# The seam into the last feed-forward stage: three engines' order written down, and some half weights in an idle staging tile

## The chip, the cores and the metric

The kernel runs on one core of a Trainium2 chip. The metric is the device time of one execution in microseconds. TensorE (PE) multiplies matrices, ScalarE (ACT), VectorE (DVE) and GpSimd (POOL) do the rest of the arithmetic, and SyncE (SP) issues most of the transfers; POOL issues the others.

## The reference

Two layers of a diffusion backbone over 1024 latent tokens of width 1024 and 256 context tokens, in float32. Layer 0 mixes with Fourier groups and long convolutions, layer 1 with neighbourhood attention; each ends with a gated feed-forward part. What matters here is the end of layer 1:

```python
def swiglu(u, w_gate, w_up, w_down):
    return (jax.nn.silu(u @ w_gate) * (u @ w_up)) @ w_down

y_lat, y_ctx = mixer_na(u_lat, u_ctx, na_w_qkv[j], na_w_out[j], na_rpb[j], not last)
h_lat = h_lat + g1 * y_lat
h_lat = h_lat + g2 * swiglu(modulate(rms_norm(h_lat, norm2_g[i]), sh2, sc2),
                            ffn_w_gate[i], ffn_w_up[i], ffn_w_down[i])
...
return rms_norm(h_lat, final_g)
```

`mixer_na` projects to queries, keys and values (the latent tokens and the keys and values of the context), attends, and multiplies by `na_w_out`. The feed-forward width is 2816, eleven pairs of 128-column blocks in each of gate and up.

## The kernel before

**Numbers.** An activation or a weight is split into two float16 tiles, a high and a low half, and a product takes three matmuls: high by high, high by low, low by high. TensorE does a 128x512 piece per matmul.

**The feed-forward products.** Gate and up products run by Strassen's scheme in Winograd's form: a 2x2 block product in seven products, A11·B11, A12·B21, S1·T1, S2·T2, S3·T3, A22·T4 and S4·B22. A and S come from the weights, B and T from the activations. Each product has four blocks of the inner dimension, so twelve matmuls. `wino_steps` is a generator that yields after each product; `Steps.to(n)` runs one to its n-th product. After products 1, 4 and 5 ScalarE copies a sum out of PSUM (`snap`); after 2, 5 and 7 VectorE adds to it. Pair i of the hidden blocks has a gate chain `g` and an up chain `up`.

**The activations' operands.** B11 and B21 come from the first half of the tokens and are there early (`wino_first`, in tiles `s4`). The others need the second half and its RMS factor: `wino_second` scales a block by that factor (`scaled`), subtracts (T1, T2, T3, T4), and makes the two halves: the high one by a cast on ScalarE, the low one by a subtraction on VectorE (`out`). It yields after each block, twenty in all, in the order T1, T2, T3, T4, B22. The high and low tiles are named `s4`, as the float32 blocks are named `s2`.

**The weights.** A pair's weights arrive in float32 in the staging tile `ws` (two buffers of 128x1024) and in others; `abs_sums` takes absolute sums on ScalarE, TensorE adds these over partitions (a 128x1 matmul), and from the scale `half_split` makes `wh` and `wl` (two buffers each). Of pairs 0 and 1 of layer 1 the halves are ready in DRAM (`d`) and are loaded to `wh` and `wl`, and S operands to `s2`. Pair 2, the third, is the first to be split there.

**The stages around the change.** After layer 0 comes the attention, whose first key weights are loaded as halves into `wh`/`wl` (`halves_of("wk", 0)`). The output projection with `na_w_out` (`w_out2`) runs as `first_part(pc)`, the first six inner blocks for token half pc, eight output blocks nb of eighteen matmuls, and `last_part(pc)`, the two remaining; `add_h` adds the residual, `square` squares and sums for the RMS norm. The seam is what follows `last_part(1)`: `rms_begin(1)` sums the squares over the partitions (small matmuls), `rms_end` makes the factor, spreads it with two matmuls and copies it to SBUF. Four chains are begun there (gate and up of pairs 0 and 1), and then `ffn` runs.

**What sets the order.** A scheduler orders the instructions of each engine from the program's text, its dependencies and its own estimate of times, and semaphores keep the data right; each engine runs its own order in sequence. Pools give buffers: a tile's load waits until the earlier tenant of its buffer has been read.

Of the kernel before, what the change touches and what calls it, by code (L numbers as in the profile page):

```python
# [12 lines left out]
F16 = mybir.dt.float16  # L13
BF16 = mybir.dt.bfloat16
AF = mybir.ActivationFunctionType
# [4 lines left out]
P = 128  # L20
# [181 lines left out]
class Builder:  # L202
    def __init__(self, ctx, tc, a, out, taps=None, stop=None):
        self.tc, self.nc, self.a, self.out = tc, tc.nc, a, out
        self.taps, self.stop = taps, stop
        ent = ctx.enter_context
        self.cp = ent(tc.tile_pool(name="cp", bufs=1))
        self.p4 = ent(tc.tile_pool(name="p4", bufs=20))
        self.p2 = ent(tc.tile_pool(name="p2", bufs=34))
        self.pg = ent(tc.tile_pool(name="pg", bufs=4))  # L210
        self.pt = ent(tc.tile_pool(name="pt", bufs=6))
        self.pko = ent(tc.tile_pool(name="pk", bufs=4))
        self.pw = ent(tc.tile_pool(name="pw", bufs=2))
        self.psum = ent(ExitStack())
        self.accumulators(pp=6, pq=2)
        self.dr = ent(tc.tile_pool(name="dr", bufs=1, space=bass.MemoryType.DRAM))
        self.pad(self.cp, PAD_C)
        self.k = self.mk = self.pk = 0
        self.banks = 8
        self.sq, self.wsc, self.uslot, self.ahead = {}, {}, {}, {}  # L220

    def pad(self, pool, w):
# [1037 lines left out]
    def abs_sums(self, tiles, st):  # L1260

        junk = self.T(BF16, 1024)
        for k, t in enumerate(tiles):
            self.nc.scalar.activation(junk[:, :t.shape[1]], t, AF.Abs, scale=2.0 ** -15, accum_out=st[:, k:k + 1])  # L1264

    def qkv_sums(self):

# [81 lines left out]
    def wino_second(self, h, l, m, r):  # L1349

        nc = self.nc
        dsh = self.C(4)
        ad = self.ucol[0]
        nc.vector.tensor_tensor(dsh, ad[:, 4:8], ad[:, 0:4], SUB)

        def out(key, j, src):
            hi, lo = self.pair((key, j))
            nc.scalar.copy(hi, src)
            nc.vector.tensor_tensor(lo, src, hi, SUB)

        ts = []

        def scaled(b):
            t = h.ap(0, b, 1)
            nc.vector.scalar_tensor_tensor(t, t, ad[:, 8 + b:9 + b], r, op0=MUL, op1=MUL)
            return t

        for j in range(4):
            t11, t21 = self.raw.pop(j), self.raw.pop(j + 4)
            t12 = scaled(j)  # L1370
            nc.vector.tensor_tensor(t11, t12, t11, SUB)
            out("T1", j, t11)
            ts.append([t11, t12, None, t21])
            yield
        for j in range(4):
            ts[j][2] = t22 = scaled(j + 4)
            t11 = ts[j][0]
            sh = ad[:, j + 4:j + 5]
            nc.vector.scalar_tensor_tensor(t11, t22, sh, t11, op0=ADD, op1=SUB)
            out("T2", j, t11)  # L1380
            yield
        for j in range(4):
            t11, t12, t22, t21 = ts[j]
            nc.vector.scalar_tensor_tensor(t12, t22, dsh[:, j:j + 1], t12, op0=ADD, op1=SUB)
            out("T3", j, t12)
            yield
        for j in range(4):
            t11, t12, t22, t21 = ts[j]
            sh = ad[:, j + 4:j + 5]
            nc.vector.scalar_tensor_tensor(t21, t21, sh, t11, op0=ADD, op1=SUB)  # L1390
            out("T4", j, t21)
            yield
        for j in range(4):
            t22 = ts[j][2]
            sh = ad[:, j + 4:j + 5]
            hi, lo = self.pair(("B22", j))
            nc.scalar.activation(hi, t22, AF.Identity, bias=sh)
            nc.vector.scalar_tensor_tensor(lo, t22, sh, hi, op0=ADD, op1=SUB)
            yield

# [91 lines left out]
        self.res = {(0, 0): c11, (0, 1): c12, (1, 1): c22, (1, 0): pa}  # L1492
        yield

    def wino_begin(self, l, i, m, tile, ctile=None):

        key = (l, i, m)
        w = self.first_ahead(key)
        s = Steps(self.wino_steps(w, tile, ctile))
        s.w, s.whole = w, False  # L1500
        s.to(2)
        return s

    def ffn(self, l, u, h, hs, second, after, keep=None, begun={}):
# [67 lines left out]
        def fetch(i, m):  # L1572
            b = begun.get((i, m))
            if i < n2 and (b is None or not b.whole):
                g = self.weights_ahead((l, i, m), b.w) if b else self.wino_weights((l, i, m))
                next(g)
                waiting[(i, m)] = g

        fetch(0, 0)
        for i in range(n2):  # L1580
            g, up = begun.get((i, 0)), begun.get((i, 1))
            if g is None or not g.whole:
                wg = waiting.pop((i, 0))
                w = next(wg)
                next(wg)
            fetch(i, 1)
            if g is None:
                g = Steps(self.wino_steps(w, self.G))
                g.to(1)
            if prev is not None:  # L1590
                prev[0].to(7)
                finish(i - 1, prev[1])
            wu = waiting.pop((i, 1))
            w = next(wu)
            if up is None:
                up = Steps(self.wino_steps(w, self.TK))
            if i == 0:
                for k, _ in enumerate(second):
                    if k == 11:
                        next(wu)  # L1600
            next(wu, None)
            fetch(i + 1, 0)
            for k in (3, 4, 5) if i == 0 and l == 1 else ():
                g.to(k)
                up.to(k)
            g.to(5)
            up.to(1)
            if i == n2 - 1:
                scales = self.down_scales(l, nh)
                if l == 0:  # L1610
                    self.qkv_scales()
            g.to(7)
            gate = dict(self.res)
            inv = self.wsc[(l, i, 0)][1]
            for k in ((0, 0), (1, 1), (0, 1)):
                nc.scalar.activation(gate[k], gate[k], AF.Silu, scale=inv)
            t = self.G()
            nc.scalar.activation(t, gate[(1, 0)], AF.Silu, scale=inv)
            gate[(1, 0)] = t
            up.to(5)  # L1620
            prev = (up, gate)
            for k in (2 * i - 2, 2 * i - 1) if l == 1 else (9, 10) if i == 9 else (i,) if i < 9 else ():
                if 0 <= k < n2:
                    sums(k)
            for _ in range(2):
                next(todo, None)
# [234 lines left out]
        for _ in range(3):  # L1861
            yield w

    def halves_of(self, n, b):

        t = [self.pw.tile([P, 1024], F16, tag=g, name=self.nm(g)) for g in ("wh", "wl")]
        for k, x in enumerate(t):
            self.ld(x, self.halves[(n, b)][:, k * 1024:(k + 1) * 1024])
        return t
# [38 lines left out]
    def attn_prep(self, pr, u):  # L1908
# [68 lines left out]
            vt.append((v, lo))  # L1977

        acc = None
        wk = self.halves_of("wk", 0) if pr == 0 else self.aw  # L1980
        for pc in (0, 1, 2):
            if pc == 1:
                wq = self.halves_of("wq", pr)
# [191 lines left out]
    def run(self):  # L2175
# [228 lines left out]

        def first_part(pc):
            for nb in range(KB):
                wh, wl = (self.pw.tile([P, 1024], F16, tag=g, name=self.nm(g)) for g in ("wh", "wl"))
                for k, x in enumerate((wh, wl)):
                    self.ld(x[:, :768], self.halves[("w_out2", nb)][:, k * 1024:k * 1024 + 768])
                if pc == 0:  # L2410
                    yield None
                acc = self.PQ() if pc == 0 else self.PS()
                for kb in range(6):
                    if pc == 0 and nb == 0:
                        load_o(kb, (0,), self.ld)
                        yield 1
                    if pc == 0 and nb == 2:
                        load_o(kb, (1,), self.ld)
                    if kb == 2:
                        load_h2(nb, pc)  # L2420
                    for w, part in ((wh, 0), (wh, 1), (wl, 0)):
                        self.mm(acc, w[:, kb * P:(kb + 1) * P], by_row(o.ap(part, kb, pc)),
                                kb == 0 and w is wh and part == 0, kb == 5 and w is wl)
                    yield 0.5
                add_h(nb, pc, acc)
# [53 lines left out]
            nc.scalar.activation(sq[:, c0:c0 + 256], h4.ap(0, KB - 1, pc), AF.Square)  # L2479
            yield from scale_out(pc, self.rms_end(pc, self.rms_begin(pc, [self.sq[1][0], sq], c0), False))  # L2480

        begun = {(0, 0): self.wino_begin(1, 0, 0, self.G)}
        c = self.rms_begin(1)
        begun[(0, 1)] = self.wino_begin(1, 0, 1, self.TK)
        r1 = self.rms_end(1, c)
        begun[(1, 0)] = self.wino_begin(1, 1, 0, self.G, self.TK)
        begun[(1, 1)] = self.wino_begin(1, 1, 1, self.TK, self.S2)
        self.ffn(1, None, h4, hs1, self.wino_second(h2, 1, 3, r1), after4, begun=begun)


def host_layout(i):
# [75 lines left out]
```

## Time and profile before

| | us |
|---|---|
| median of three runs | 2901.01 |
| lowest, highest | 2895.24, 2902.95 |
| profiled execution | 2897.71 |
| its span | 2895.6 |
| TensorE busy in it | 2758.4 (95%) |
| VectorE, ScalarE, GpSimd busy | 2081.9, 1620.2, 593.0 |

The mean granted clock of TensorE was 0.978 of full speed. A row of a timeline gives start, duration, engine, line, operation and tiles (out<-in), shape and count, and in brackets how long the engine stood before it and what released it. `SPq` is a transfer issued by SP. Lines are those of the kernel before; in the kernel after the same lines stand 1 to 26 further down.

### The profile page before, as it was taken

The page shows a single profiled execution, that of the slowest core. Times are in us where ns is not written, and L with a number is a line of the kernel's source. Part 1 is how long each engine was busy: PE and PEld are TensorE (multiplying, and loading weights), DVE is VectorE, ACT ScalarE, POOL GpSimd, SP SyncE. Part 2 cuts the span into 40 slices and gives each one's busy share as a digit, 9 for nine tenths or more (in the row PEclk, how much of TensorE's full clock was granted, in tenths as well). Part 3 has the DMA queues.
Part 4 walks back from the last instruction along what each step waited for, and adds up shares of the span by engine and source line. Part 5 has one row for each costly group of instructions (what it writes and reads, how often), then busy time and mean ns, then how long its engine had stood idle before and what let it go on. Part 6 is the DMA issues. An engine that isn't in the chain of part 4 may idle for free. (4 is left out here: it accounts for less than half of the span.)

```text
span 2895.6 us, 46377 instructions
## 1 busy us (share of the span) xinstructions
PE 2758.4 (95%) x16419; PEld 1688.7 (58%) x16419; DVE 2081.9 (72%) x3857; ACT 1620.2 (56%) x2857; POOL 593.0 (20%) x977
## 2 busy tenths in 40 slices
PE   6989999999989999999999999999999899999998
PEld 3766557878879644444555844666664444444554
DVE  4778867585467798877886777777775778775755
ACT  4664325453675666654555555666663567554543
POOL 1012013354220111123120012343321112112000
PEclk8989999999999999999999999999999999999999
DMA  7574435358785655566995698777864756425753
GB/s 257 191 275 161 159 124 159 109 165 293 279 342 177 211 209 196 201 221 219 315 336 193 238 330 333 167 170 167 177 186 166 248 199 246 151 95 184 237 190 117
DMA packets 323363, 607.60 MB, mean 210 GB/s; under 512 B 89910, under 2 KB 131576, under 8 KB 323130
## 3 DMA queue, kind: packets, MB, share of 16 engines
q1 hardware_dynamic: 254682, 387.53, 41.6%
q0 software_dynamic: 66144, 212.91, 20.8%
q10 hardware_dynamic: 2304, 4.20, 0.4%
q8 instruction: 129, 2.11, 0.3%
q14 instruction: 104, 0.85, 0.1%
HBM read 455.33 MB, written 135.53 MB: 204 GB/s over the span
## 5 line engine op out<-in xcount | busy, mean ns | idle before, releaser
L1462 PE MATMUL ps<-s,s 128*128 128x512 f16 x2244 | 507.3, 381 | 8.9 <-ACT g L1467 4.7
L1462 PEld LDWEIGHTS <-s 128*128 128x128 f16 x2640 | 258.7, 98 | 332.3 <-issue 26.8
L296 PE MATMUL ps<-s,wh 128*128 128x256 f32 (+3 forms) x1764 | 402.3, 331 | 12.1 <-ACT wh L300 5.7
L1231 ACT ACTIVATE s<-s,c 128x512 f16<-128x512 f32 (+1 forms) x324 | 233.2, 752 | 147.3 <-DMA s<-d 71.4
L1232 DVE SCALAR_TENSOR_TENSOR s<-s,c,s 128x512 f16<-128x512 f32 (+1 forms) x324 | 247.3, 792 | 87.0 <-ACT s L1231 85.9
L1679 PE MATMUL ps<-s 128*128 128x512 f16 (+2 forms) x1308 | 303.8, 378 | 2.3 <-DVE s L1232 2.0
L296 PE MATMUL pq<-s,wh 128*128 128x512 f16 (+1 forms) x988 | 271.4, 352 | 5.0 <-DMA wh<-d 3.0
L296 PE MATMUL ps<-s,wl 128*128 128x256 f32 (+3 forms) x882 | 264.4, 332 | 2.6 <-DMA wl<-d 1.6
L1679 PEld LDWEIGHTS <-s 128*128 128x128 f16 x1536 | 148.4, 98 | 179.5 <-issue 7.4
L296 PEld LDWEIGHTS <-wh 128*128 128x128 f16 x1664 | 159.1, 99 | 151.1 <-issue 12.2
L287 POOL DMA_DIRECT2D d<-s x201 | 108.6, 541 | 652.2 <-DVE s L1523 186.1
L348 ACT CAST mat<-cs 128x1024 fp32r<-128x1024 f16 (+2 forms) x120 | 111.5, 934 | 140.5 <-PE ps L296 53.5
L296 PEld LDWEIGHTS ps<-s,wh 128*128 128x128 f32 x1088 | 178.3, 193 | 18.4 <-ACT wh L300 5.9
L296 PE MATMUL ps<-s,mat 128*128 128x512 f32 x696 | 183.1, 410 | 3.1 <-DVE s L302 2.8
L1462 PE MATMUL ps<-s,wh 128*128 128x512 f16 x608 | 182.3, 379 | 1.6 <-DVE g L1476 1.2
L296 PE MATMUL pq<-s,wl 128*128 128x512 f16 (+1 forms) x494 | 171.2, 352 | 0.0
L296 PEld LDWEIGHTS <-s 128*128 128x128 f16 x2400 | 113.6, 98 | 80.7 <-issue 12.8
L296 PEld LDWEIGHTS ps<-s,mat 128*128 128x128 f32 x696 | 135.7, 197 | 37.1 <-DVE s L302 3.2
L1264 ACT ACTIVATE t<-s 128x1024 bf16<-128x1024 f32 (+1 forms) x164 | 141.5, 864 | 13.4 <-DVE c L483 8.6
L296 PE MATMUL sc<-s,s 128*128 128x65 f16 (+3 forms) x2688 | 142.6, 231 | 3.2 <-ACT t L2080 2.4
L296 PEld LDWEIGHTS <-wl 128*128 128x128 f16 x832 | 81.8, 99 | 81.2 <-DMA wl<-d 2.5
L1231 ACT ACTIVATE s<-t,c 128x512 f16<-128x512 f32 x172 | 115.2, 712 | 21.9 <-DVE c L1330 9.3
(435 smaller groups left out, 5505.9 us busy)
## 6 DMA issues: line engine op xcount, KB each, us to landing
s<-d SPq DMA_DIRECT2D x294, 256.0 KB, 4.2
d<-s POOLq DMA_DIRECT2D x157, 256.0 KB, 3.7
s<-in_down SPq DMA_DIRECT2D x154, 256.0 KB, 5.0
s<-in_ada_w POOLq DMA_DIRECT2D x48, 512.0 KB, 4.9
s<-in_gate SPq DMA_DIRECT2D x46, 512.0 KB, 4.0
s<-in_up SPq DMA_DIRECT2D x46, 512.0 KB, 3.8
d<-g POOLq DMA_DIRECT2D x87, 256.0 KB, 3.4
d<-tk POOLq DMA_DIRECT2D x82, 256.0 KB, 4.9
```

The source lines that it names most:

```text
L287: self.last_ldr = self.nc.gpsimd.dma_start(out, in_).ins
L296: return self.nc.tensor.matmul(o, l, r, start=st, stop=sp).ins
L348: self.nc.scalar.copy(m, st)
L1231: nc.scalar.activation(hi, src, AF.Copy, scale=scale)
L1232: nc.vector.scalar_tensor_tensor(lo, src, scale, hi, op0=MUL, op1=SUB)
L1264: self.nc.scalar.activation(junk[:, :t.shape[1]], t, AF.Abs, scale=2.0 ** -15, accum_out=st[:, k:k + 1])
L1462: nc.tensor.matmul(ps, x[:, sl], y, start=first and j == 0 and x is wh and y is xh, stop=j == 3 and x is wl, skip_group_check=True)
L1679: m = nc.tensor.matmul(acc[j][:, c0:c1], x[:, sl], y[:, xs], start=first and k == 0, stop=last and k == 2, skip_group_check=True)
```

## The change

**Staging tile.** The key weights of the attention's first head pair, and the halves of `w_out2` for even nb in `first_part(1)`, go to a buffer of the tag `ws`, high half in its first 1024 columns and low half in the others. The transfers of SP move with the buffers. SP ahead of the attention, before (`d_3522` holds the first key weights, `d_3526` the first query weights, `in_gate` and `in_up` the float32 weights of the third pair):

```order
L281 DMA ws_5399_25751<-in_gate 128x1024
L281 DMA s4_3749_17455<-in_up 128x1024
L281 DMA s4_3750_17456<-in_up 128x1024
L281 DMA ws_5433_25949<-in_up 128x1024
L281 DMA wl_3815_17559<-d_3522_16515 128x1024
L281 DMA wh_3814_17558<-d_3522_16515 128x1024
```

and after (`d_3644` holds `w_out2`'s block 0):

```order
L282 DMA ws_3814_17558<-d_3522_16515 128x1024 x2
L282 DMA s4_3749_17455<-in_up 128x1024
L282 DMA s4_3750_17456<-in_up 128x1024
L282 DMA ws_5024_24831<-d_3644_16969 128x768 x2
L282 DMA wl_3819_17599<-d_3526_16522 128x1024
L282 DMA wh_3818_17598<-d_3526_16522 128x1024
```

The key weights stand where the first staging load stood, and the two staging loads `ws<-in_gate` and `ws<-in_up` have moved behind `first_part(1)`'s last load and into `last_part(1)`'s. At the start of the attention the scheduler also puts ScalarE's first value cast behind the context keys' scores; the steady part of the attention reads as before.

**Seam.** From the first of the four chains to the end of pair 0's gate activation the order on PE, ACT and DVE is that of the program's text, not the scheduler's. The text runs the RMS chain between product 1 and product 2 of the first gate chain, gives one block of `wino_second` at a time between the products, and then S1·T1 of gate and up, S2·T2 of both, S3·T3 of both with further blocks between. The low half of a block is subtracted one block later than its cast. `abs_sums` keeps behind the last cast of B22.

ScalarE from the RMS factor to T1's casts, before (`st` and `t` carry the factor, g and tk are products of chains, L1264 is `abs_sums`, L1358 a cast):

```order
L527 ACTIVATE st_5099_25245<-ps_5098_25240,c_9_95 128x4
L1616 ACT_TABLE_LOAD
L1616 ACTIVATE g_5096_25224<-g_5096_25224,c_5_93 128x512
L538 ACTIVATE t_5105_25281<-c_1_86,st_5099_25245 128x128 x4
L1467 COPY tk_5103_25265<-ps_5102_25252 128x512
L1264 ACTIVATE t_5398_25735,c_7_94<-g_5096_25224 128x512
L1264 ACTIVATE t_5402_25756,st_5401_25755<-ws_5399_25751 128x1024
L542 COPY t_5105_25281<-ps_5106_25286 128x512
L1467 COPY tk_5110_25306<-ps_5109_25293 128x512
L1358 CAST s4_5371_25500<-s2_5036_24885 128x512
```

and after:

```order
L528 ACTIVATE st_5093_25228<-ps_5092_25223,c_9_95 128x4
L539 ACTIVATE t_5095_25245<-c_1_86,st_5093_25228 128x128 x4
L543 COPY t_5095_25245<-ps_5096_25250 128x512
L1478 COPY tk_5100_25270<-ps_5099_25257 128x512
L1363 CAST s4_5103_25276<-s2_5034_24883 128x512
L1363 CAST s4_5103_25276<-s2_5040_24917 128x512
L1363 CAST s4_5105_25298<-s2_5047_24952 128x512
L1478 COPY tk_5109_25318<-ps_5108_25305 128x512
L1363 CAST s4_5105_25298<-s2_5053_24986 128x512
L1633 ACT_TABLE_LOAD
```

The table load with its Silu, and the two absolute sums, have gone from the RMS chain; the sums follow thirty rows further down, behind the last B22 cast. VectorE makes the operands from the factor. Its order before, from the last scale of the second half on (`s2` blocks, L1365 scale, L1371 T1, L1384 T3, L1359 low half):

```order
L1365 SCALAR_TENSOR_TENSOR s2_5072_25077<-s2_5072_25077,c_1927_8040,t_5105_25281 128x512
L1371 TENSOR_TENSOR s2_5036_24885<-s2_5028_24843,s2_5036_24885 128x512
L1371 TENSOR_TENSOR s2_5043_24920<-s2_5038_24890,s2_5043_24920 128x512
L1371 TENSOR_TENSOR s2_5050_24955<-s2_5045_24925,s2_5050_24955 128x512
L1476 TENSOR_TENSOR tk_5110_25306<-pq_5111_25308,tk_5110_25306 128x512
L1371 TENSOR_TENSOR s2_5057_24990<-s2_5052_24960,s2_5057_24990 128x512
L1384 SCALAR_TENSOR_TENSOR s2_5028_24843<-s2_5059_24995,c_5369_25496,s2_5028_24843 128x512
L1384 SCALAR_TENSOR_TENSOR s2_5038_24890<-s2_5064_25025,c_5369_25496,s2_5038_24890 128x512
L1359 TENSOR_TENSOR s4_5371_25500<-s2_5036_24885,s4_5371_25500 128x512
```

and after, from the first scale on:

```order
L1372 SCALAR_TENSOR_TENSOR s2_5026_24841<-s2_5026_24841,c_1927_8040,t_5095_25245 128x512
L1378 TENSOR_TENSOR s2_5034_24883<-s2_5026_24841,s2_5034_24883 128x512
L1372 SCALAR_TENSOR_TENSOR s2_5036_24888<-s2_5036_24888,c_1927_8040,t_5095_25245 128x512
L1378 TENSOR_TENSOR s2_5040_24917<-s2_5036_24888,s2_5040_24917 128x512
L1364 TENSOR_TENSOR s4_5103_25276<-s2_5034_24883,s4_5103_25276 128x512
L1487 TENSOR_TENSOR tk_5100_25270<-ps_5104_25282,tk_5100_25270 128x512
L1372 SCALAR_TENSOR_TENSOR s2_5042_24922<-s2_5042_24922,c_1927_8040,t_5095_25245 128x512
L1378 TENSOR_TENSOR s2_5047_24952<-s2_5042_24922,s2_5047_24952 128x512
L1364 TENSOR_TENSOR s4_5103_25276<-s2_5040_24917,s4_5103_25276 128x512
```

Before, all eight blocks are scaled first, and parts of T3 are made ahead of T1's low halves. After, a block is scaled when its operand is due, and its low half follows one block later, with the additions of products (L1487) between.

The diff, cut to its core:

```diff
     def abs_sums(self, tiles, st):
         junk = self.T(BF16, 1024)
-        for k, t in enumerate(tiles):
-            self.nc.scalar.activation(junk[:, :t.shape[1]], t, AF.Abs, scale=2.0 ** -15, accum_out=st[:, k:k + 1])
+        with self.follow(self.behind):
+            for k, t in enumerate(tiles):
+                self.nc.scalar.activation(junk[:, :t.shape[1]], t, AF.Abs, scale=2.0 ** -15,
+                                          accum_out=st[:, k:k + 1])
...
+        late = []
         def out(key, j, src):
             hi, lo = self.pair((key, j))
             nc.scalar.copy(hi, src)
-            nc.vector.tensor_tensor(lo, src, hi, SUB)
+            late.append(lambda: nc.vector.tensor_tensor(lo, src, hi, SUB))
+            if l == 0 or len(late) > 1:
+                late.pop(0)()
...
-            nc.scalar.activation(hi, t22, AF.Identity, bias=sh)
+            last = nc.scalar.activation(hi, t22, AF.Identity, bias=sh).ins
+            if l == 1:
+                self.behind = last
+            if late:
+                late.pop(0)()
...
-            if i == 0:
+            if i == 0 and begun:
+                fetch(1, 0)
+                next(second)
+                for k in (3, 4, 5):
+                    g.to(k)
+                    up.to(k)
+                    for _ in range(3 if k == 5 else 4):
+                        next(second)
+            elif i == 0:
                 for k, _ in enumerate(second):
...
-            fetch(i + 1, 0)
-            for k in (3, 4, 5) if i == 0 and l == 1 else ():
-                g.to(k)
-                up.to(k)
+            if i or not begun:
+                fetch(i + 1, 0)
...
             up.to(5)
+            if i == 0:
+                self.seam.close()
...
+    def half_pair(self, spare):
+        if spare:
+            t = self.pw.tile([P, 2048], F16, tag="ws", name=self.nm("ws"))
+            return t[:, :1024], t[:, 1024:]
+        return [self.pw.tile([P, 1024], F16, tag=g, name=self.nm(g)) for g in ("wh", "wl")]
...
-        wk = self.halves_of("wk", 0) if pr == 0 else self.aw
+        wk = self.halves_of("wk", 0, True) if pr == 0 else self.aw
...
-                wh, wl = (self.pw.tile([P, 1024], F16, tag=g, name=self.nm(g)) for g in ("wh", "wl"))
+                wh, wl = self.half_pair(pc == 1 and nb % 2 == 0)
...
-        begun = {(0, 0): self.wino_begin(1, 0, 0, self.G)}
+        e = mybir.EngineType
+        self.seam.enter_context(self.tc.manual_schedule(engines={e.PE, e.Activation, e.DVE}))
+        g = self.wino_begin(1, 0, 0, self.G, None, 1)
         c = self.rms_begin(1)
-        begun[(0, 1)] = self.wino_begin(1, 0, 1, self.TK)
-        r1 = self.rms_end(1, c)
-        begun[(1, 0)] = self.wino_begin(1, 1, 0, self.G, self.TK)
-        begun[(1, 1)] = self.wino_begin(1, 1, 1, self.TK, self.S2)
-        self.ffn(1, None, h4, hs1, self.wino_second(h2, 1, 3, r1), after4, begun=begun)
+        g.to(2)
+        second = self.wino_second(h2, 1, 3, self.rms_end(1, c))
+        up = self.wino_begin(1, 0, 1, self.TK, None, 1)
+        next(second)
+        next(second)
+        up.to(2)
+        next(second)
+        g1 = self.wino_begin(1, 1, 0, self.G, self.TK, 1)
+        next(second)
+        g1.to(2)
+        next(second)
+        up1 = self.wino_begin(1, 1, 1, self.TK, self.S2, 1)
+        next(second)
+        next(second)
+        up1.to(2)
+        next(second)
+        begun = {(0, 0): g, (0, 1): up, (1, 0): g1, (1, 1): up1}
+        self.ffn(1, None, h4, hs1, second, after4, begun=begun)
```

`self.seam` is an ExitStack that holds the manual order open until pair 0's gate activation; `self.behind` starts as None, and `wino_begin` has a new argument `to` that says after which product it stops (2 as before where it isn't given).

More of the change, by code (lines that the diff above doesn't have):

```diff
@@ L219, in __init__ @@
         self.banks = 8
+        self.seam, self.behind = ExitStack(), None
         self.sq, self.wsc, self.uslot, self.ahead = {}, {}, {}, {}
@@ L1493, in wino_steps, with wino_begin @@
         yield
-    def wino_begin(self, l, i, m, tile, ctile=None):
+    def wino_begin(self, l, i, m, tile, ctile=None, to=2):
         key = (l, i, m)
@@ L1500, in wino_begin @@
         s.w, s.whole = w, False
-        s.to(2)
+        s.to(to)
         return s
@@ L1862, in weights_ahead, with halves_of @@
             yield w
-    def halves_of(self, n, b):
-        t = [self.pw.tile([P, 1024], F16, tag=g, name=self.nm(g)) for g in ("wh", "wl")]
+    def half_pair(self, spare):
[3 more added lines that the diff above has]
+        return [self.pw.tile([P, 1024], F16, tag=g, name=self.nm(g)) for g in ("wh", "wl")]
+    def halves_of(self, n, b, spare=False):
+        t = self.half_pair(spare)
         for k, x in enumerate(t):
```

## The prediction

> **What bounds the kernel now.** I read the page's list of busy time first, then the waits of TensorE by place, then the timelines around each wait, and last the clock in stretches of 5 us.
>
> ```profile
> PE 2758.4 (95%) x16419; PEld 1688.7 (58%) x16419; DVE 2081.9 (72%) x3857; ACT 1620.2 (56%) x2857; POOL 593.0 (20%) x977
> ```
>
> TensorE is busy for 95% of the span, with the same 25,542 instructions in its order before and after. A gain can only come from its idle stretches and from stretches at a low clock. Its waits from 2200 to 2400 us (what was waited for, total us, times, longest):
>
> ```profile
> PE pq L1462 <- ACT s L1358: 4.2, 1, 4.2
> PE pq L1462 <- DVE tk L1476: 3.1, 1, 3.1
> PE pq L1462 <- ACT tk L1467: 2.9, 1, 2.9
> ...
> PE pq L1462 <- DVE c L1329: 1.2, 1, 1.2
> ...
> PE ps L1462 <- ACT g L1467: 0.5, 1, 0.5
> ```
>
> Two groups stand here: operands and a bank at the start of the last feed-forward stage (4.2 and 3.1), and the weights of its third pair (2.9, 1.2, 0.5). Two more places, where TensorE waits for a DMA, follow with parts 1 and 2.
>
> **Part 1: the key weights in the staging tile.** SP's issues, and TensorE where it waits for them:
>
> ```profile
> 1762.71 0.33 SPq L281 DMA_DIRECT2D ws<-in_gate  x1
> 1770.22 0.33 SPq L281 DMA_DIRECT2D ws<-in_up  x1
> 1770.64 0.40 SPq L281 DMA_DIRECT2D wl<-d  x1
> 1771.10 0.47 SPq L281 DMA_DIRECT2D wh<-d  x1
> 1780.78 0.61 PE L296 MATMUL pq<-s,wh 128*128 128x512 f16 x2 [2.99 <-DMA wh<-d]
> ```
>
> The first key weights go out at 1770.64 and 1771.10 and TensorE stands 2.99 us for them. After, they take the slot of `ws<-in_gate` in SP's order: 8.4 us sooner (1771.10 - 1762.71). Were the transfer as slow as now (at most 1780.78 - 1771.10 = 9.7 us), it lands by 1772.4, 5.4 us before TensorE is free (1780.78 - 2.99 = 1777.8). The two staging loads (512 KB each) also leave this saturated stretch. Late next is the PSUM bank: the order moves the first value cast behind the context keys on ScalarE, and I price what is left at 0.3 us, half of one 0.61-us row. The bounds are 0 (another transfer late in the same place) and -3.0. I take **-2.7 us**, near the wait's own row.
>
> **Part 2: w_out2's even blocks in the staging tile.** First half of the sum over blocks, second token half:
>
> ```profile
> 2214.71 0.39 PE L296 MATMUL ps<-s,wl 128*128 128x512 f16 x1 [0.38 <-DMA wl<-d]
> 2219.82 0.60 PE L296 MATMUL ps<-s,wh 128*128 128x512 f16 x2 [0.68 <-DMA wh<-d]
> 2221.61 0.39 PE L296 MATMUL ps<-s,wl 128*128 128x512 f16 x1 [1.19 <-DMA wl<-d]
> ```
> ```profile
> 2209.83 0.32 SPq L281 DMA_DIRECT2D wh<-d  x1
> 2213.71 0.32 SPq L281 DMA_DIRECT2D wh<-d  x1
> ```
>
> The waits sum to 2.25 us. The loads go out only as one of two buffers comes free (2209.83, 2213.71), some 6 us ahead of use, while the DMA engines are full:
>
> ```profile
> 2215.00:2220.00 5.00, 4.32 (x25) 1.00 0.96 358
> 2220.00:2225.00 5.00, 3.81 (x18) 1.00 0.32 118
> ```
>
> (Columns: length, TensorE busy with its count, granted clock, DMA share, GB/s.) Two pairs of buffers double the lead, ahead of the burst. What it moves here are the two 512-KB staging loads: 1.05 MB at 358 GB/s is 2.9 us of DMA. In SP's order they stand behind the last w_out2 block, and from 2220 on the engines are at 0.32, so they should hide; if they fall ahead of needed weights they cost up to 2.9 us. SP's wait for the staging slot (block 4 done) is shorter than that of the issue just ahead of it (block 5 done), so it holds up nothing. Bounds -2.25 and +2.9; I take **-2.0**.
>
> **Part 3: the seam.** The chain of the RMS factor, then the operands made from it, on ScalarE, VectorE and TensorE:
>
> ```profile
> 2257.43 0.69 DVE L514 TENSOR_TENSOR tk<-tk,tk 128x512 f32<-128x512 f32 x1 [0.16 <-ACT tk L509]
> 2260.90 0.95 PE L296 MATMUL ps<-c,tk 128*128 128x1 f32 x8
> 2262.16 1.28 ACT L1616 ACT_TABLE_LOAD   x1
> 2263.46 0.72 ACT L1616 ACTIVATE g<-g,c 128x512 f32<-128x512 f32 x1
> 2264.09 1.26 ACT L538 ACTIVATE t<-c,st 128x128 f32<-128x128 f32 x4
> 2267.96 1.02 PE L296 MATMUL ps<-t,c 128*128 128x512 f32 x2
> 2269.30 1.04 ACT L1264 ACTIVATE t<-ws 128x1024 bf16<-128x1024 f32 x1
> 2270.34 0.56 ACT L542 COPY t<-ps 128x512 f32<-128x512 f32 x1
> ```
> ```profile
> 2276.24 1.89 DVE L1371 TENSOR_TENSOR s<-s,s 128x512 f32<-128x512 f32 x3
> 2278.78 0.59 PE L1462 MATMUL pq<-s,wh 128*128 128x512 f16 x2 [3.10 <-DVE tk L1476]
> 2285.75 0.59 PE L1462 MATMUL pq<-s,s 128*128 128x512 f16 x1 [4.22 <-ACT s L1358]
> 2329.11 2.75 PE L1462 MATMUL ps<-s,s 128*128 128x512 f16 x12 [0.49 <-ACT g L1467]
> 2334.72 4.44 PE L1462 MATMUL pq<-s,s 128*128 128x512 f16 x12 [2.86 <-ACT tk L1467]
> ```
>
> Before, the squares are summed at 2258.1 (2257.43 + 0.69), but TensorE sums over partitions only at 2260.90, ScalarE puts a table load and a Silu (1.28 + 0.72) and later an absolute sum (1.04) ahead, and VectorE has the factor at 2270.9 (2270.34 + 0.56). After: the small matmuls (0.95) stand right behind the first product, to 2259.1; the second product (twelve matmuls, 2.75 us by the row at 2329.11) runs to 2261.9; broadcast 1.02 and copy 0.56: **2263.5, 7.4 us sooner**. Both table load and Silu are behind three casts now and delay none of the chain.
>
> VectorE then makes T1 block by block: scale, difference, low half, three steps of 0.63 (three L1371 take 1.89). Four blocks take 7.6, three additions of products between them 1.9, lags of the casts perhaps 1: T1 is complete by 2274.0. TensorE, without the 3.10, comes to S1·T1 at 2278.4 (2285.75 - 4.22 - 3.10): 4.4 us in hand. T2 takes twelve more steps, 7.6, and two additions, 1.3: 2282.9; its last block is needed at 2278.4 + 2 x 2.75 + 2.0 = 2285.9: 3 us in hand. The later three operands have 1.9 us a block at most against a product of 2.75 per bank. So no operand wait is left. What is late next is the bank of the fourth early pair: its addition stands on VectorE behind up to two operand steps. Bounds 0 and today's 3.1; I take 1.0, nearer the lower end, since two such steps are 1.3 us. The 7.3 us (3.10 + 4.22) become 1.0: **-6.3**.
>
> The clock. Same columns as before:
>
> ```profile
> 2285.00:2290.00 5.00, 4.25 (x11) 0.50 0.00 0
> 2290.00:2295.00 5.00, 5.00 (x23) 0.91 0.67 176
> 2335.00:2340.00 5.00, 5.00 (x18) 0.66 0.37 135
> 1780.00:1785.00 5.00, 4.22 (x20) 1.00 1.05 406
> ```
>
> Right after the 4.22-us wait TensorE runs at half rate: 4.25 x 0.50 + 5 x 0.09 = 2.6 us lost. With no wait above 1 us this goes: **-2.6** (bounds 0 and -2.6). After the 2.86-us wait 5 x 0.34 = 1.7 us are lost, but after the 2.99-us wait at 1780.78 the clock stays at 1.00. So about 3 us idle can do either.
>
> [...]
>
> **The third pair's weights.** TensorE reaches them 6.3 + 2.6 = 8.9 us sooner. ScalarE does not:
>
> ```profile
> 2301.50 1.07 ACT L1264 ACTIVATE t<-s 128x1024 bf16<-128x1024 f32 x1
> 2312.57 1.14 ACT L1231 ACTIVATE wh<-ws,c 128x1024 f16<-128x1024 f32 x1
> 2325.87 0.59 PE L1462 MATMUL pq<-s,wh 128*128 128x512 f16 x2 [1.16 <-DVE c L1329]
> ```
>
> From the first of the absolute sums after the operands to the split of the weight passes 11.1 us. After the change all sums stand behind the last B22 cast, the two that were done at 2268.7 too (0.63 + 1.04 and their readouts, about 2 us). B22 itself waits on TensorE's order, so that I put the first sum at about 2302, and the split at 2302 + 11.1 + 2 = 2315; with 1.14 for the high half and a like time for the low half on VectorE the weights stand at 2317.5. TensorE wants them at 2325.87 - 1.16 - 8.9 = 2315.8: 1.7 us, in place of 1.16; the next product is behind in the same way. All in all I put 5.6 us for today's 4.5 (1.16 + 0.49 + 2.86): **+1.1**; bounds -2 (the sums start at 2299) and +8.9 (nothing of ScalarE's work comes sooner). Since these waits are shorter each, I take the clock's loss of 1.7 at 1.0: **-0.7**.
>
> Sum: -2.7 - 2.0 - 6.3 - 2.6 + 1.1 - 0.7 = **-13.2 us**. The profiled execution took 2897.71 (span 2895.6 and 2.1 around it), so 2884.5 for one like it; it lies 3.3 below the median of the runs, 2901.01, from which I count: 2887.8, say 2888. A measurement of this kernel can tell about 0.3%, 8.7 us.
>
> **Rivals.** *Given back at the third pair* (no change). If ScalarE's sums begin no sooner and each later cast queues behind them, the +8.9 bound holds: -13.2 - 1.1 + 8.9 = -5.4, 2895.6. For it: the 11.1 us stand in a row on ScalarE, and the sums can't pass the last cast. Against: before, they began only when TensorE's next result let them, and that comes 8.9 us sooner. It decides if the split starts after about 2319.
>
> *The other transfers stay late* (no change in parts 1 and 2). DMA is at 1.0 around 1780; if the value tokens or the query weights become the late ones, and the staging loads press w_out2's last blocks, 4.7 us go: 2892.5, at the edge.
>
> *Slower: the attention.* Its order is drawn anew by the scheduler behind the changed buffers, over the 400 us between the two places quoted in parts 1 and 2. The first rows differ (value casts behind context keys), the steady ones read alike. To be 0.3% slower it has to lose 13.2 + 8.7 = 22 us, 2.7 us in each of eight head pairs; half of that leaves no change. At 3 us a pair: 2888 + 24 = 2912. It decides if TensorE waits over 2.7 us a pair for keys or values.
>
> *The operands come sooner for nothing.* S1's weights are loaded behind the fourth pair's:
>
> ```profile
> 2267.71 22.20 SPq L281 DMA_DIRECT2D s<-d  x18
> s<-d SPq DMA_DIRECT2D x294, 256.0 KB, 4.2
> ```
>
> TensorE wants them at 2278.4 rather than 2285.7. Issued from 2267.7 on, with the page's median of 4.2 us to landing and six loads of 256 KB ahead (0.73 us each at 358 GB/s), the last that S1·T1 needs lands at 2276.3: 2 us in hand. If they are later by 6 us, a wait of 4 and the half rate behind it (2.6) come back: -13.2 + 3 + 2.6 = -7.6, 2893.4.
>
> **Chances.** The sum as forecast 0.66; given back 0.11; transfers late 0.09; S1's weights late 0.06; attention 0.08. Faster by over 0.3% (below 2892.3) are the first but for 0.05 where its smaller terms fall short together (4.5 us are in hand), half of the transfers (0.05) and a third of S1's weights (0.02): 0.68. Slower is the attention but for 0.01: 0.07. The rest, 0.25, is the same within 0.3%. The range: all low bounds together, -3.0 - 2.25 - 7.3 - 2.6 - 2 - 1.7 = -18.9, give 2882, and 2 us for the spread of the runs 2880; upward it takes in the rivals that end in no change (2895.6) with their spread, 2899, and leaves out the attention.
>
> **What would show it.** Right: no wait of TensorE for the first key weights; L542's copy by 2264 on the old scale, or about 7 us after the last square; no wait for T1's casts; clock 1.00 through S1·T1; one group of waits at the third pair's split, about 5 to 6 us in all. Wrong: waits there near 13 us, a DMA named at S1·T1, or waits spread over the attention.

## The result and the profile after

| | before | after |
|---|---|---|
| first comparison, median (runs) | 2900.93 (4) | 2877.34 (4) |
| its ratio, 95% interval | | 0.992 (0.9901 to 0.994) |
| repeated (E1), median (runs) | 2894.42 (23) | 2878.56 (6) |
| its ratio, 95% interval | | 0.9945 (0.9929 to 0.9962) |
| these runs and E4's, mean | 2896.4 (39) | 2877.7 (10) |
| profiled execution, span | 2897.71, 2895.6 | 2880.55, 2878.8 |

Faster, by 23.6 us in the comparison that the forecast is measured by and by 18.7 us between the means in the table (19.5 with all other runs on record: 2896.8 in 53, 2877.3 in 11); the forecast was 13.2 us and 2888. TensorE's waits from 2180 to 2400 us in the kernel after:

```profile
PE pq L1473 <- DVE wl L1233: 1.8, 1, 1.8
PE pq L1473 <- ACT g L1478: 1.6, 2, 1.4
PE tr L2126 <- DVE s L2138: 1.1, 1, 1.1
PE pq L1473 <- ACT wh L1232: 1.0, 1, 1.0
PE ps L1473 <- ACT g L1478: 1.0, 1, 1.0
PE pq L1473 <- DVE tk L1487: 0.9, 1, 0.9
```

The 4.2 for an operand's cast and the waits for w_out2's DMA are gone, the wait for a PSUM bank (the 3.1, "the bank" from here on) is 0.9, and the longest is 1.8. The clock in the four places (length, TensorE busy, granted clock, DMA share, GB/s):

```profile
1760.00:1800.00 40.00, 39.55 (x194) 1.00 0.94 361
2200.00:2240.00 40.00, 40.00 (x189) 1.00 0.61 210
2265.00:2290.00 25.00, 24.15 (x113) 1.00 0.90 320
2305.00:2330.00 25.00, 21.12 (x99) 1.00 0.81 294
```

Full speed in all four; before, 2285 to 2290 was at 0.50 ("half rate" from here on) and 2335 to 2340 at 0.66. SP and TensorE at the staging tile's two uses:

```profile
1761.71 0.88 SPq L282 DMA_DIRECT2D ws<-d  x2
1776.97 13.34 PE L297 MATMUL pq<-s,ws 128*128 128x512 f16 x72 [0.17 <-ACT tk L1919]
2228.36 0.33 SPq L282 DMA_DIRECT2D ws<-in_gate  x1
```

The key weights go out 15 us ahead of use, and the third pair's staging load after the burst of transfers. The RMS chain and the operands, on VectorE, TensorE and ScalarE:

```profile
2251.89 0.69 DVE L515 TENSOR_TENSOR tk<-tk,tk 128x512 f32<-128x512 f32 x1 [0.16 <-ACT tk L510]
2252.77 0.95 PE L297 MATMUL ps<-c,tk 128*128 128x1 f32 x8
2254.27 1.28 ACT L539 ACTIVATE t<-c,st 128x128 f32<-128x128 f32 x4 [0.25 <-DVE st L530]
2256.17 1.02 PE L297 MATMUL ps<-t,c 128*128 128x512 f32 x2
2257.23 0.59 ACT L543 COPY t<-ps 128x512 f32<-128x512 f32 x1 [1.68 <-PE ps L297]
2269.71 0.69 DVE L1364 TENSOR_TENSOR s<-s,s 128x512 f16<-128x512 f32 x1
2273.58 5.34 PE L1473 MATMUL ps<-s,s 128*128 128x512 f16 x24
2278.27 0.68 DVE L1364 TENSOR_TENSOR s<-s,s 128x512 f16<-128x512 f32 x1
2278.76 2.75 PE L1473 MATMUL pq<-s,s 128*128 128x512 f16 x12
```

The factor is there 5.2 us after the last square (2257.82 less 2252.58), against 12.8 before. T1's last low half ends at 2270.4, ahead of S1·T1 at 2273.6; T2's ends at 2278.95 (its row is the fourth of T2), when S2·T2 has begun at 2278.76 but wants it only for its last block, 1.95 us later: 1.8 us in hand.

The 4.2 before was not what the prediction took it for. These are VectorE, ScalarE and TensorE around it in the kernel before (L1379 makes T2):

```profile
2283.70 0.68 DVE L1359 TENSOR_TENSOR s<-s,s 128x512 f16<-128x512 f32 x1
2284.30 2.07 DVE L1379 SCALAR_TENSOR_TENSOR s<-s,c,s 128x512 f32<-128x512 f32 x3
2285.08 6.10 ACT L1358 CAST s<-s 128x512 f16<-128x512 f32 x11 [2.93 <-DVE s L1379]
2285.75 0.59 PE L1462 MATMUL pq<-s,s 128*128 128x512 f16 x1 [4.22 <-ACT s L1358]
2286.13 7.90 PE L1462 MATMUL ps<-s,s 128*128 128x512 f16 x25
```

The cast that ends the wait is T2's first. The matmul at 2285.75, one alone into the bank of the gate chain's first product, is the first of S2·T2; the scheduler had put it ahead of S1·T1, which is 24 of the 25 matmuls behind it. T1's low halves were made from 2280.57 to 2284.38 (the first ended at 2281.25), and TensorE stood from 2281.53 on. Had S1·T1 come first, T1 would have cost it some 0.7 us, by an estimate from these rows. The written order has S1·T1 of both chains first.

### The profile page after: what moved, and what is told of

Same layout as the page of the kernel before. It is cut to its first block, busy times and chain, and to the rows that moved or that the text cites. A ratio compares the mean times of both kernels' runs of the same rounds, so it can differ in the third digit from the quotient of the medians.

```text
span 2878.8 us, 46360 instructions
## 1 busy us (share of the span) xinstructions
PE 2751.2 (96%) x16419; PEld 1684.7 (59%) x16419; DVE 2082.7 (72%) x3857; ACT 1620.5 (56%) x2857; POOL 594.4 (21%) x977
## 5 line engine op out<-in xcount | busy, mean ns | idle before, releaser
L297 PE MATMUL ps<-s,wh 128*128 128x256 f32 (+3 forms) x1716 | 387.0, 329 | 11.1 <-ACT wh L301 5.4
L297 PE MATMUL pq<-s,wh 128*128 128x512 f16 (+1 forms) x940 | 259.2, 352 | 2.0 <-ACT wh L1232 1.7
L297 PE MATMUL ps<-s,wl 128*128 128x256 f32 (+3 forms) x858 | 254.6, 330 | 1.3 <-DVE wl L303 1.2
L297 PEld LDWEIGHTS <-wh 128*128 128x128 f16 x1568 | 149.8, 99 | 138.1 <-issue 12.5
L297 PEld LDWEIGHTS ps<-s,wh 128*128 128x128 f32 x1088 | 177.7, 192 | 18.1 <-ACT wh L301 5.7
L297 PE MATMUL pq<-s,wl 128*128 128x512 f16 (+1 forms) x470 | 162.9, 352 | 0.0
L1233 DVE SCALAR_TENSOR_TENSOR s<-t,c,s 128x512 f16<-128x512 f32 x172 | 123.4, 745 | 1.6 <-ACT s L1232 1.6
```

The costliest lines, as they stand in the source:

```text
L297: return self.nc.tensor.matmul(o, l, r, start=st, stop=sp).ins
L1233: nc.vector.scalar_tensor_tensor(lo, src, scale, hi, op0=MUL, op1=SUB)
```

## The experiments

Beside the timed runs I compare traces by stretches, each from the start of one matmul to the start of a later one, counted in TensorE's order (16,419 matmuls in every kernel): the **key weights** from the 8990th to the 9100th, **w_out2**'s second half from the 13,200th to the 13,478th, the **seam** from the 13,606th to the 13,900th, which holds the third pair's first products. All times are us.

| trace | key weights | w_out2 | seam |
|---|---|---|---|
| before, the first | 24.35 | 55.25 | 79.69 |
| before, E4 | 25.72 | 58.24 | 78.54 |
| before, E8 | 25.80 | 54.98 | 78.92 |
| before, E9 | 26.03 | 55.68 | 78.93 |
| before, E10 | 26.03 | 55.42 | 80.20 |
| **mean of before** | **25.59** | **55.91** | **79.26** |
| after | 21.71 | 52.49 | 68.32 |
| after, E1 | 21.71 | 52.49 | 68.31 |
| after, E11 | 21.71 | 52.49 | 68.77 |
| E2, seam only | 24.35 | 57.04 | 69.54 |
| E3, halves only | 21.71 | 52.49 | 75.62 |
| E5, RMS later | 21.71 | 52.49 | 71.72 |
| E6, no deferral | 21.71 | 52.49 | 76.39 |
| E7, sums later | 21.71 | 52.49 | 72.35 |

Mean before less mean after (68.47 in the seam): 3.88 + 3.42 + 10.79 = **18.1 us**.

**E1, the changed kernel again.** No edit.

> The changed kernel once more. Theory A (the gain sits in the places named and nowhere else): the two traces, laid beside each other matmul by matmul, give 2.8 us at the first key weights, 2.8 at w_out2, 11.8 in the seam and -0.4 behind it, 17 us in all (ratio 0.994), and the rest of the 23.6 us between the medians is chance in the part ahead of 1760 us, where both programs are the same. Theory B (the change also quickens the part ahead of it): 23 us again (0.992), and its trace is again 1 us or more ahead at 1762 us.

Ratio 0.9945, 15.9 us between the medians. Between A's 17 and B's 23 it is nearer A, and its interval (0.9929 to 0.9962) leaves B's 0.992 out. Ahead of 1762 us its trace is 0.4 us ahead of the first trace of before (1767.63 against 1768.03 to the 8990th matmul), not 1 or more.

**E2, the seam alone.**

```diff
-        wk = self.halves_of("wk", 0, True) if pr == 0 else self.aw
+        wk = self.halves_of("wk", 0) if pr == 0 else self.aw
...
-                wh, wl = self.half_pair(pc == 1 and nb % 2 == 0)
+                wh, wl = self.half_pair(False)
```

> The order of the seam alone, all half weights in wh and wl as before. The prediction's terms for part 3: -6.3 - 2.6 + 1.1 - 0.7 = -8.5 us. Theory A by the trace of the changed kernel: -11.8 us (7.3 us of waits to 0.9, both stretches at half rate gone, 4.3, third pair 4.5 to 3.9). Rival: the seam is worth more only together with the halves, and alone is -8.5 or less. The waits of 3.0 and 2.3 us for halves by DMA stay in its trace.

Ratio 0.9969 (0.9956 to 0.9981), 9.0 us with an interval from 5.5 to 12.7, too wide to tell 8.5 from 11.8. The trace tells it: 69.54 against 79.26, 9.7 us. (It has 3.4 us at half rate at the third pair, which the first two traces of the changed kernel, 68.32 and 68.31 in the seam, lack.) The waits for halves are there as expected:

```profile
PE pq L297 <- DMA wh<-d: 3.0, 1, 3.0
...
PE ps L297 <- DMA wl<-d: 1.5, 2, 1.0
...
PE ps L297 <- DMA wh<-d: 0.9, 1, 0.9
```

**E3, the halves alone.** The kernel before with `half_pair` and its two uses.

> The half weights in the staging tile alone, the seam by the scheduler as before. Theory A: -2.7 - 2.0 = -4.7 by the prediction, -5.6 by the trace; waits of 4.2, 3.1 and 2.9 us stay. Rival: the two absolute sums that the scheduler has early in the seam now wait for the staging loads that were moved, and the gain is lost there: 0.

Ratio 0.9962 (0.9948 to 0.9976): 11.0 us, twice what either theory said. The key weights and w_out2 give 7.3 by the table; the seam gives 3.6 more, though nothing of its text was changed. Its waits from 2240 us on:

```profile
PE pq L1462 <- DVE tk L1476: 3.1, 1, 3.1
PE pq L1462 <- ACT tk L1467: 2.9, 1, 2.9
...
PE pq L1462 <- DVE s L1359: 0.7, 1, 0.7
```

The 4.2 is gone, and the 0.7 is for a low half of T2. VectorE's order up to T1's last low half is the one of before, and so is the RMS chain with its table load and sums; what differs is TensorE's order. With other buffers the scheduler put the gate chain's S1·T1 ahead of the first matmul of S2·T2:

```profile
2278.00 2.75 PE L1462 MATMUL ps<-s,s 128*128 128x512 f16 x12
2280.70 0.38 PE L1462 MATMUL pq<-s,s 128*128 128x512 f16 x1
2280.91 2.97 PE L1462 MATMUL ps<-s,s 128*128 128x512 f16 x13
```

So the wait for an operand goes without an earlier factor; the bank's 3.1 does not. Neither outcome was expected (4.2 stays; the gain is lost at the sums). The parts do not add (9.7 + 10.9 in the traces, 18.1 together): the written order replaces what the scheduler would have gained by itself.

**E4, the kernel before against itself,** and **E8 to E10, three more traces of it; E11, one more of the changed kernel.** No edits.

> The kernel before against itself: what the measurement makes of no change. Both theories: ratio 1.000, within 0.2%. Its trace shows whether the half-rate stretches at 1649 and 1714 us, which the changed kernel's trace lacks, come in every execution (then theory B gains) or in some (theory A).

> The kernel before, for its trace. Theory C (each wait of 2 to 4 us puts TensorE at half rate in some executions and not in others, so that the change is worth the waits and the mean of what the half rate costs behind them): from execution to execution the same stretch differs; from the matmul ahead of the first key weights over 110 matmuls 24.4 us without and about 26 with a half-rate stretch, over w_out2's second half 55.3 without and 57 to 58 with. Among three more traces at least one more has the half rate behind w_out2's waits or the key weights. Rival: the first trace (24.4 and 55.3) is what the kernel does, and the one seen later was an outlier.

> The same once more: the same two outcomes for each of the stretches.

> The same a third time. Over all traces of the kernel before, the mean of the stretches less that of the changed kernel is 3 us for the key weights, 4 for w_out2 and 11 for the seam, 18 in all, by theory C; 2.7, 2.8 and 11 by the rival.

> The changed kernel a third time, for its trace. Theory C: with no wait over 1.8 us between 1760 and 2400 us there is no half rate there, and the stretches are within 0.3 us of the first two traces (21.7, 52.5 and 68.3 us).

E4's ratio is 1.0013 (0.9999 to 1.0026), its twelve runs from 2884.86 to 2906.42. Of the half-rate stretches at 1649 and 1714 us that E4 was to look for, E4 has one 8 us earlier and half as long as the first, and none like the second: they come and go. (On the axis of the rows shown here the two lie from 1638.9 and from 1703.8 us on; the first trace has a clock of 0.89 from 1630 to 1660 and of 0.89 from 1700 to 1715, the first of the changed kernel 1.00 in both.) More to the point is the clock at the key weights, in the first trace and in E10's, and at w_out2, in the first trace and in E4's:

```profile
1776.00:1800.00 24.00, 21.01 (x110) 1.00 0.90 335
2210.00:2235.00 25.00, 22.75 (x108) 1.00 0.53 182
```
```profile
1776.00:1800.00 24.00, 21.02 (x93) 0.93 1.03 404
```
```profile
2210.00:2235.00 25.00, 22.50 (x93) 0.86 0.52 181
```

The same 3.0-us wait ahead of the key weights: no half rate in the first execution (1.00 over 24 us), and in the other four, at 0.93, 24 x 0.07 = 1.7 us lost, 3.4 at half rate. At w_out2 one execution in five lost 25 x 0.14 = 3.5, seven us at half rate: the clock is 1.00 up to 2221, when a wait of 1.5 us ends, and 0.50 behind it, where a wait of 1.0 follows. E2's kernel has TensorE's and SP's order of before in both places, so that its trace is a sixth execution of them: no half rate at the key weights (24.35), and 3.4 us of it at w_out2 (57.04) behind waits of 0.9 and 1.0. With it the means are 25.38 and 56.10, and the 18.1 stays. In the seam all five have it (0.86 of 25 us, 2275 to 2300), although the operand's wait was 4.2 in two executions and 2.5 to 2.6 in three. In these three one of two stretches at half rate fell between the bank's wait and the operand's, which it shortened by as much as it cost, 1.7 us: from 2275 to 2300 TensorE is busy for 19.3 to 19.4 us there, against 17.7 in the other two. Theory C holds for the key weights; at w_out2 none of the three new traces has it, so the 4 us expected there are 3.4, and 2.8 without E4's. The changed kernel had none between 1760 and 2400 in two traces and one of about 3.5 us in E11 (25 x 0.07 = 1.75 lost, 2295 to 2320), at the third pair's waits of 1.0 and 1.8. That one was not expected: theory C had taken waits of 1.8 us and less to be harmless, and E11's seam is 0.45 us longer than the first.

The length of a wait does not tell here whether the clock falls: half rate followed waits of 2.5 to 3.0 us (clock 0.93 over 24 us at the key weights in E4 and E8 to E10, 0.86 over 25 us in the seam), of 1.5 in E4 (0.86 over 25 us), of 0.9 and 1.0 in E2 (57.04 against 55.25 in the table) and of 1.0 and 1.8 in E11 (0.93 over 25 us), while it did not follow those of 3.0 in the first trace (1.00 over 24 us) and in E2 (24.35 in both). What decides it is not shown.

**E5, the RMS chain two products later.**

```diff
-        c = self.rms_begin(1)
         g.to(2)
-        second = self.wino_second(h2, 1, 3, self.rms_end(1, c))
         up = self.wino_begin(1, 0, 1, self.TK, None, 1)
-        next(second)
-        next(second)
+        c = self.rms_begin(1)
         up.to(2)
+        second = self.wino_second(h2, 1, 3, self.rms_end(1, c))
+        g1 = self.wino_begin(1, 1, 0, self.G, self.TK, 1)
```

and the blocks of `wino_second` behind it in turn.

> The changed kernel with the RMS chain two products later on TensorE: the small matmuls behind the first product of the up chain, the factor behind its second, so some 5.3 us later. By the trace of the changed kernel T1 is complete 5.1 us ahead of its last use and T2 3.0 us. Theory (the gain of the seam is the lead that the early chain gives VectorE): about 0.2 us of wait at T1 and 2.3 at T2, 2 to 3 us of the gain lost, no half rate: -14 us against before (0.995). Rival: the operands have slack enough, nothing lost (0.9945). Second rival: the additions of products in VectorE's line feed the delay back, 5 us or more lost and the half rate with it: -9 us or less.

The seam is 3.3 us longer (71.72 less 68.47), about the size of the theory, but in another place. VectorE, then TensorE:

```profile
2260.50 0.68 DVE L1487 TENSOR_TENSOR tk<-pq,tk 128x512 f32<-128x512 f32 x1
2261.24 0.59 PE L1473 MATMUL pq<-s,wh 128*128 128x512 f16 x2 [3.91 <-DVE tk L1487]
```

No operand was late: TensorE stood at the bank that the fourth chain begins in, and the addition that frees it stood behind operand steps on VectorE, without a gap. That wait is 3.91 in place of 0.9. (The 3.0 us that this expectation and the next have in hand at T2 are those of its third block; by the fourth they are 1.8.) The runs (0.9935, 0.9917 to 0.9952) are too wide to show 3 us.

**E6, low halves not deferred.**

```diff
-            if l == 0 or len(late) > 1:
+            if len(late) > 0:
```

> The changed kernel with each low half subtracted right behind its cast, not one block later. Theory: VectorE then stands about 0.7 us per block for ScalarE's cast, 2.8 us by the end of T1 (5.1 in hand), 5.6 by the end of T2 (3.0 in hand), 8.4 by T3: waits of TensorE of some 2.6 us at T2 and 2 at T3, 4 to 6 us of the gain lost, -11 us against before (0.996). Rival: the lead of the early chain covers it, nothing lost.

Ratio 0.9954 (0.9939 to 0.9969) against 0.996 expected; in the seam 7.9 us are lost (76.39), against 4 to 6. VectorE stands 0.7 us at each block for the cast, as expected, and again the bank is what TensorE meets first:

```profile
2266.33 0.69 DVE L1364 TENSOR_TENSOR s<-s,s 128x512 f16<-128x512 f32 x1 [0.68 <-ACT s L1363]
2266.94 0.68 DVE L1487 TENSOR_TENSOR tk<-pq,tk 128x512 f32<-128x512 f32 x1
2267.68 0.59 PE L1473 MATMUL pq<-s,wh 128*128 128x512 f16 x2 [3.64 <-DMA s<-d]
```

The trace names a DMA, but the addition ends at 2267.62, 0.06 us before the matmul, as in E5. No wait at T2 or T3, as far as the trace lists them; the rest is in copies of products (1.57 and 1.44) and at the third pair (2.90 and 1.51), with a half-rate stretch of 3.4 us there (from 2317.2 to 2320.6 two matmuls take up to 1.06 in place of 0.59).

**E7, the sums of the down weights behind the third pair's split.** `half_split` keeps its cast in `self.cut`.

```diff
+                if l == 1 and i == 2:
+                    self.behind = self.cut
+                    sums(0)
+                    sums(1)
                 next(wg)
...
-            for k in (2 * i - 2, 2 * i - 1) if l == 1 else (9, 10) if i == 9 else (i,) if i < 9 else ():
+            for k in (2 * i - 2, 2 * i - 1) if l == 1 and i != 1 else (9, 10) if l == 0 and i == 9 else (i,) if l == 0 and i < 9 else ():
```

> The changed kernel with the absolute sums of the first two down weights kept behind the split of the third pair's weight, which then stands eleven rows sooner on ScalarE. Theory (the 3.9 us of waits at the third pair are ScalarE's queue of sums ahead of the split): those waits fall to 1 us or less, -19 us against before (0.9935). Rival: the sums that move back are ahead of the copies and casts that TensorE wants next, the waits only move, and nothing is gained (0.9945).

The rival holds. ScalarE and TensorE:

```profile
2300.06 1.13 ACT L1232 ACTIVATE wh<-ws,c 128x1024 f16<-128x1024 f32 x1
2307.84 0.56 ACT L1478 COPY g<-ps 128x512 f32<-128x512 f32 x1
2308.45 5.28 PE L1473 MATMUL ps<-s,s 128*128 128x512 f16 x12 [5.36 <-ACT g L1478]
```

The split comes sooner and the wait at it goes, but a product's copy now stands behind the moved sums: 5.36 us in one piece, and the next twelve matmuls take 5.28 in place of 2.75, at half rate (granted clock 0.83 from 2300 to 2320). The seam is 3.9 us longer (72.35); the runs (0.9945, 0.9926 to 0.9964) do not tell it from E1. No version tried beats the changed kernel.

One part of the change seems to do nothing: by the orders as I read them, every engine's instructions stand the same with or without `follow` in `abs_sums`. No run shows it.

## Why the prediction was wrong

It gave 2888 where 2877.3 was measured, below its range of 2880 to 2899, and 13.2 us of gain where 23.6, or 18.7 over all runs, were. The places and the earlier factor held. Three sizes and the base did not, and one wait was read wrongly, which luck covered. The 10.5 us between 2887.8 and 2877.3 are 4.6 of the base, 5.5 of the terms (18.7 less 13.2) and 0.4 between median and mean of the kernel after.

- **The base.** I counted from 2901.01, the median of three runs. The mean of 39 is 2896.4, 4.6 lower, while the median of the changed kernel's first four runs (2877.3) lies at its mean (2877.7). So some 5 of the 23.6 us lie in the first runs of before, and the low end of the range, which allowed 2 us for the spread, was too near. Chance or not is open: E1 to E7 ran on chip 14 and E8 to E11 on chip 0, and the record has no chip for the first comparison. The kernel before has a mean of 2896.1 in 46 runs on chip 14, 2902.2 in three on chip 0 and 2900.0 in the first four, so that a difference between chips is not excluded.
- **Part 1, sized at -2.7:** 3.9. The wait went as worked out (2.99 to 0.17), and the bank's 0.3 was 0.2. The failed step is "after the 2.99-us wait at 1780.78 the clock stays at 1.00": true of that execution, not of the kernel. Four of five executions lost some 1.7 us behind the wait (four of six with E2's), 1.2 in the mean of the table.
- **Part 2, sized at -2.0:** 3.4 by the mean of the traces. The waits went whole, 2.25 and no remnant; they were 1.4 to 2.8 in other executions, and one had the half rate, for which this part had no term at all. The staging loads hid, as argued (issued at 2228.36, and TensorE without a wait in that stretch).
- **Part 3, the chain:** forecast 5.4 us from the last square to the factor (2263.5 less 2258.1), measured 5.2. T1 was complete 3.2 us ahead of S1·T1, against 4.4, and T2 had 1.8 in hand, against 3. No operand wait. The bank's wait was sized at 1.0 and was 0.9, but not for the reason given, an addition behind two operand steps: VectorE stood 0.58 us for the product and added at once, and TensorE began as that addition ended.

```profile
2267.66 0.69 DVE L1487 TENSOR_TENSOR tk<-pq,tk 128x512 f32<-128x512 f32 x1 [0.58 <-PE pq L1473]
2268.40 0.59 PE L1473 MATMUL pq<-s,wh 128*128 128x512 f16 x2 [0.85 <-DVE tk L1487]
```

  That the number fits is luck. E5 and E6 show that the bank, not an operand, is what the lead protects there.
- **Part 3, the 4.22 us:** the failed step is to take the row at 2285.75 for S1·T1 and its wait for a late T1. It was the first matmul of S2·T2, waiting for T2's first cast in a place that TensorE's order gave it. The 7.3 us became 0.85, close to the forecast, but the 4.2 of it did not need the earlier factor. In E3 it went with the factor as late as before and TensorE's order changed; in E5, in the written order, it stayed away with the factor 10.4 us after the last square (5.2 in the changed kernel, 12.8 before). That the sum came out is luck too. No run moves that one matmul by itself.
- **The clock, -2.6 and -0.7:** both went whole in two traces of three; the second term was 1.0 short there. E11 and E2, whose seam is the same, have a stretch at half rate at the third pair (3.4 us in E2, about 3.5 in E11, where the clock is 0.93 over 25 us).
- **The third pair, +1.1:** the term with the wrong sign. The waits fell from 4.5 to 3.9 (1.03 + 1.83 + 1.02), -0.6. ScalarE's part was right:

```profile
2297.00 0.63 ACT L1266 ACTIVATE t<-g 128x512 bf16<-128x512 f32 x1 [0.36 <-DVE g L1568]
2309.87 1.13 ACT L1232 ACTIVATE wh<-ws,c 128x1024 f16<-128x1024 f32 x1
2311.06 0.60 PE L1473 MATMUL pq<-s,wh 128*128 128x512 f16 x2 [1.03 <-ACT wh L1232]
2313.50 0.39 PE L1473 MATMUL pq<-s,wl 128*128 128x512 f16 x1 [1.83 <-DVE wl L1233]
2316.85 2.75 PE L1473 MATMUL ps<-s,s 128*128 128x512 f16 x12 [1.02 <-ACT g L1478]
```

  From the first sum to the split pass 12.9 us against 13.1 forecast (11.1 + 2). The wait at the split itself was longer than forecast (2.86 against 1.7). What I had not worked out was the rest: I put 3.9 for it (5.6 less 1.7, "behind in the same way"), and it was 1.02, since the copy that TensorE had waited for (tk, eight rows behind g's in ScalarE's order, with the next weight's split between) now stands right behind g's.

The seam in all: 10.8 measured against 8.5. With 3.9 and 3.4 that is 18.1, which with the runs' 18.7 leaves 0.6. Of the rivals, the loss at the third pair, late transfers and S1's weights did not come; in the attention the stretch from the 9100th to the 13,200th matmul took 387.2 to 388.6 us after, against 387.7 to 389.2.

What stays open: ahead of the 8990th matmul, where both programs are the same, the five traces of before took 1766.3 to 1775.0 us (mean 1769.5) and the three of the changed kernel 1759.4 to 1767.6; with those of E2, E3 and E5 to E7, whose matmuls up to there are the same too, eight took 1758.2 to 1768.9 (mean 1763.9). The 18.7 us need no difference there, the 23.6 of the first comparison would. I can't tell it from chance.

## What to carry to other kernels

Price a wait of TensorE by the wait and by the mean of what half rate costs behind it (3.0 and 1.2 us at the key weights here), and take that mean over several profiles of the same kernel: one profile shows one draw. Count a forecast from more than three runs where their spread is as large as the gain. When operands are made by an engine that also empties PSUM, look for the first late bank as well as for the first late operand, and don't add up parts that a scheduler orders anew. Before a wait is put down to a late operand, work out which product the waiting matmul belongs to (its bank, and the line that made what it waits for): the cure may be the order of the waiting engine.

## What was not expected of the hardware

The same wait of 3.0 us (2.7 in E4) was followed by 3.4 us at half rate in four executions (clock 0.93 over 24 us) and by none in a fifth (1.00) and in E2's, and a wait of 1.5 us, with one of 1.0 behind it, by about 7 us of it in one (0.86 over 25 us). The spread of one and the same kernel was 21.6 us in twelve runs (2884.86 to 2906.42), more than the change is worth.
